# Raw weights asked for five products sooner, and one bank copied out by ScalarE, in the Strassen stage of a hybrid encoder block

## The chip, the cores and the metric

The kernel runs on one core of one Trainium2 chip. The metric is the device time of one execution in microseconds. The core has TensorE (PE, matmuls), VectorE (DVE), ScalarE (ACT), GpSimd (POOL) and SyncE (SP, which here issues nearly all DMAs). Each engine works through a queue of its own in order; they meet through semaphores.

## The reference, cut to what matters

The block takes a sequence of 1024 tokens of width 1024, normalises and modulates it to h, projects h with a wide matrix, runs a gated short convolution (branch a) and a bidirectional gated DeltaNet (branch b), and merges both. For this change only the projections for branch a and the last gates matter:

```
proj = h @ w_in[l]
(a_bg, a_cg, a_x, a_z, q, k, v, z_b, a_raw, b_raw, gate_a_raw, gate_b_raw) = jnp.split(proj, ...)
ya = a_cg * dwconv_centred(a_bg * a_x, conv_a_w[l])
ya = ya * jax.nn.silu(a_z)
ya = ya @ w_pa[l]
...
merged = jax.nn.sigmoid(gate_a_raw) * ya + jax.nn.sigmoid(gate_b_raw) * yb
```

## The kernel before, in words

Weights and h are kept as pairs of a high and a low part, so that one product becomes three matmuls (hi·hi, hi·lo, lo·hi). A projection's 1024 columns are eight tiles of 128 columns.

The DeltaNet part comes first. Then, from about 762 us to 1120 us of the span, the *Strassen stage* computes eighteen pairs of column tiles: for j = 0, 2, 4, 6 the pairs bg, ax, cg, az (`a_bg`, `a_x`, `a_cg`, `a_z`), and then the gates gb2 and gb4. Each pair (class `Pair`) is a 2 x 2 block product done with seven products in place of eight (Strassen-Winograd). A product is 12 matmuls of 128x128 by 128x512. The seven are called S2, A11, S1, S3, A12, A22, S4 after their weight operand; A11 to A22 are quarters of the raw weights, S1 to S4 sums of them (VectorE, line 1308). The pair bg0 has the place "first" and another order of products, the pair gb4 the place "last".

For each product there are these steps:
- `load` (line 1317): SyncE asks for the pair's four raw quarters, 256 KB each, into a ring of eight raw buffers, so two pairs' worth.
- `prep`: the sum, if the operand is one, and ScalarE's copy into the high part (line 1324), both five products ahead (`AHEAD = 5`). `prep` calls `load` when a raw quarter is first needed.
- `rest`: VectorE's subtraction into the low part (line 1331), four products ahead.
- `product` (line 1343): the matmuls. S2 and S3 go to a bank of one pool, S1 and S4 to a bank of another; S3 adds into the bank that already holds S2.
- `after`: what leaves the banks. `e1` is ScalarE's copy of A11's bank (line 1349), `u2` is S2's bank plus `e1` (VectorE, line 1351). TensorE may begin S3 only when `u2` has been read from that bank.

`steps` is the list of all products in order; near its end two entries are exchanged, so that gb4's S2 comes one product sooner, ahead of gb2's S4. The order of every engine's instructions in this stage is the order in which this code issues them. The products of branch a are multiplied together by VectorE into a tile `a`, and SyncE stores it to `y_d` (line 1426), one store per column tile, after the last product of az. In the profile a tile's name has no numbers: `u_bg`, `S_gb`, `wr_gb` stand for `u2_bg0`, `S1_gb4`, `wr_gb4..` and their likes; `whS`, `whiS`, `whA`, `whiA` are high parts, `wlS` and so on low parts.

Of the kernel before, what the change touches and what calls it, by code (L numbers as in the profile page):

```python
# [11 lines left out]
ALU = mybir.AluOpType  # L12
# [19 lines left out]
AHEAD = 5  # L32
# [295 lines left out]
def block(ctx: ExitStack, tc: tile.TileContext, x, c, wada, wadag, badaT, nwT, win, wab, cva, cvq,  # L328
# [3 lines left out]
    V, S, G, Q = (Engine(sched, n, e) for n, e in (("dve", nc.vector), ("act", nc.scalar), ("pool", nc.gpsimd),  # L332
                                                   ("dma", nc.sync)))

    def pool(name, bufs, **kw):
        return ctx.enter_context(tc.tile_pool(name=name, bufs=bufs, **kw))
# [4 lines left out]
    pg = pool("pg", 2, space=PSUM)  # L341
# [899 lines left out]
    V, S, G, Q, PE = nc.vector, nc.scalar, nc.gpsimd, nc.sync, nc.tensor  # L1241
# [4 lines left out]
    def wtile(src, name):  # L1246
        hi = wp.tile([P, KT * P], F32R, tag="whi", name=f"wh_{name}")
        lo = wp.tile([P, KT * P], F32R, tag="wlo", name=f"wl_{name}")
        for q in range(2):
            raw = wp.tile([P, 512], F32, tag="wraw", name=f"wr_{name}_{q}")  # L1250
            Q.dma_start(raw, src[:, ch(q, 512)])
            S.activation(hi[:, ch(q, 512)], raw, AF.Copy)  # L1252
            G.tensor_tensor(lo[:, ch(q, 512)], raw, hi[:, ch(q, 512)].bitcast(F32), ALU.subtract)  # L1253
        return hi, lo
# [35 lines left out]
    class Pair:  # L1290
# [62 lines left out]
        def after(self, n, ps):  # L1353
            u = self.u
            if self.place == "last":
                if n in ("S2", "S3"):
                    self.temp({"S2": "u2", "S3": "u3"}[n], ps, None)
                elif n == "A11":
                    self.temp("e1", ps, None)
                    V.tensor_tensor(u["u3"], u["u3"], u["e1"], ALU.add)  # L1360
                    self.consume(1, 1, self.banks[pc], u["u3"])
                    self.consume(1, 0, self.banks[pg], u["e1"])
                    V.tensor_tensor(u["u2"], u["u2"], u["e1"], ALU.add)
                    V.tensor_tensor(u["u2"], self.banks[pc], u["u2"], ALU.add)
                elif n == "A12":
                    self.consume(0, 0, ps, u["e1"])
                elif n == "S4":
                    self.consume(0, 1, ps, u["u2"])
                return
            first = self.place == "first"  # L1370
            if n == "A11":
                self.temp("e1", ps, None)
            if n == ("S2" if first else "A11"):
                self.temp("u2", self.banks[pg], u["e1"])
                if first:
                    V.tensor_tensor(u["u2"], self.banks[po], u["u2"], ALU.add)
            if n == "S3":
                self.temp("u3", ps, u["e1"])
                self.consume(1, 1, self.banks[pc], u["u3"])
            elif n == "A12":  # L1380
                self.consume(0, 0, ps, u["e1"] if first else None)
            elif n == "A22":
                self.consume(1, 0, ps, u["e1"])
            elif n == ("S1" if first else "S4"):
                self.consume(0, 1, ps, u["u2"])
# [45 lines left out]
    def conv3(acc, b, j, i):  # L1431
        x, c = xpads[b][:, 1 + i : 1 + i + T], cva_t[:, j, i : i + 1]
        if i:
            V.scalar_tensor_tensor(acc, x, c, acc, ALU.mult, ALU.add)
        else:
            V.tensor_scalar(acc, x, c, None, ALU.mult)
# [21 lines left out]
    steps = [(p, n) for p in pairs for n in p.order]  # L1458
# [15 lines left out]
        pairs[0].after(n, early[n])  # L1474
    steps[AHEAD - 1][0].prep(steps[AHEAD - 1][1])
    for i, (p, n) in enumerate(steps):
        if i + AHEAD < len(steps):
            q, k = steps[i + AHEAD]
            q.prep(k)
        if i + AHEAD <= len(steps):  # L1480
            q, k = steps[i + AHEAD - 1]
            q.rest(k)
        p.product(n)
        if late:
            conv3(*late.pop(0))
        if i + 4 == len(steps):
            tctx.close()
            yp = ctx.enter_context(tc.tile_pool(name="yp", bufs=1, reuse_waits="tile", side="right"))
            yhi = [yp.tile([P, T], F32R, name=f"yhi{k}") for k in range(KT)]
            ylo = [yp.tile([P, T], F32R, name=f"ylo{k}") for k in range(KT)]  # L1490
            ws = [wtile(win[G_B + j], f"gb{j}") for j in (6, 7)]
            for k in range(KT):
                Q.dma_start(ylo[k].bitcast(F32), y_d[k])
# [187 lines left out]
def build(nc, arrays, dbg=None, **kw):  # L1681
    aps = {n: nc.dram_tensor(f"in_{n}", a.shape, mybir.dt.from_np(a.dtype), kind="ExternalInput").ap()
           for n, a in arrays.items()}
    out = nc.dram_tensor("out_0_dram", (1, 1024, 1024), F32, kind="ExternalOutput").ap()
    with tile.TileContext(nc, **kw) as tc:
        block(tc, *aps.values(), out, **({"dbg": dbg} if dbg else {}))
# [11 lines left out]
```

## Time and profile before

| | us |
|---|---|
| median of 3 runs (lowest, highest) | 1413.46 (1412.38, 1415.14) |
| the profiled execution's own time | 1415.61 |
| its span, first to last instruction | 1413.9 |
| PE busy | 1369.3 |
| DVE busy | 863.0 |
| ACT busy | 613.1 |
| POOL busy | 479.2 |
| mean granted TensorE clock | 0.991 |

Times inside the profile count from the start of the span. A row of a timeline is: start, duration, engine, line, operation, output and inputs, shapes, count, and in brackets the idle time of the engine before it with what ended it. SPq, ACTq, DVEq and PEq are the engines' sequencers, which issue DMAs and wait for semaphores. A row of the waits is: who waited, for whom, total, times, longest.

### The profile page before, as it was taken

How to read it: one execution, taken by the hardware profiler on the slowest of the kernel's cores; microseconds unless marked ns; L12 is line 12 of the kernel's file. 1: busy time of each engine (PE TensorE's matmuls, PEld its weight loads, DVE VectorE, ACT ScalarE, POOL GpSimd, SP SyncE). 2: the span in 40 equal slices, each digit the busy share in tenths (PEclk: the TensorE clock that was granted, in tenths of full speed). 3: DMA queues.
4: the chain of work that ended last, by engine and by line, in shares of the span. 5: the costliest groups of instructions: out<-in, count | busy, mean ns of one | idle time of the engine just before them, and what ended most of it. 6: DMA issues, size and time to landing. Idle time of an engine off the chain costs nothing.

```text
span 1413.9 us, 22356 instructions
## 1 busy us (share of the span) xinstructions
PE 1369.3 (97%) x8498; PEld 1144.7 (81%) x8498; DVE 863.0 (61%) x1479; ACT 613.1 (43%) x1495; POOL 479.2 (34%) x718
## 2 busy tenths in 40 slices
PE   6899999999999999999998999999998999999998
PEld 5678888887888888888887888888886788888886
DVE  6868175667668675857675766767676354432335
ACT  5447575564647475655534232322323331222211
POOL 2004837574747565665510000000000122455301
PEclk9999999999999999999999999999999999999999
DMA  9315341515042332314223102030301477664502
GB/s 356 97 53 161 112 92 67 150 38 143 31 99 82 83 98 71 109 46 98 54 105 120 59 38 97 16 123 26 120 30 60 172 282 246 217 205 158 178 15 104
DMA packets 124300, 155.96 MB, mean 110 GB/s; under 512 B 74657, under 2 KB 75041, under 8 KB 124194
## 3 DMA queue, kind: packets, MB, share of 16 engines
q1 hardware_dynamic: 123762, 153.24, 33.7%
q8 instruction: 66, 1.08, 0.3%
q10 hardware_dynamic: 432, 1.31, 0.2%
q14 instruction: 40, 0.33, 0.1%
HBM read 125.02 MB, written 29.50 MB: 109 GB/s over the span
## 4 chain that ended last, share of the span: by engine, by line
PE 91%; DVE 4%; DMA 1%; ACT 1%; issue 1%; SPq 0%; POOL 0%; POOLq 0%; DVEq 0%; ACTq 0%
PE pp_ga L214 6%; PE pp_z L214 6%; PE cb L214 6%; PE pp_q L214 5%; PE pp_v L214 5%; PE pp_k L214 5%; PE ps_ax_S L1343 4%; PE ps_cg_S L1343 4%; PE o L214 4%; PE ps_bg_S L1343 4%; PE ps_az_S L1343 4%; PE pp_pb L1261 2%; PE pp_pb L1263 2%; PE pp_pa L1263 2%; PE pp_pa L1262 2%; PE pp_pa L1261 2%
## 5 line engine op out<-in xcount | busy, mean ns | idle before, releaser
L1253 POOL TENSOR_TENSOR wl_gb<-wr_gb,wh_gb 128x512 fp32r<-128x512 f32 x4 | 5.1, 1296 | 360.1 <-ACT wh_gb L1252 360.1
L322 POOL TENSOR_TENSOR E<-E,et 128x30 f32<-128x30 f32 (+7 forms) x240 | 117.0, 488 | 16.8
L322 POOL TENSOR_TENSOR et<-E 128x30 f32<-128x30 f32 (+7 forms) x240 | 112.8, 470 | 29.3 <-DMA E<-s 12.7
L322 DVE SCALAR_TENSOR_TENSOR S<-S,exps,cb 128x128 f32<-128x128 f32 x96 | 29.6, 343 | 59.4 <-PE cb L214 58.8
L322 ACT ACTIVATE vw<-cb,cols 128x128 f32<-128x128 f32 x112 | 36.2, 364 | 68.2 <-PE cb L214 67.9
L214 PE MATMUL pp_z<-hhi,wh_z 128*128 128x512 f32 x128 | 52.8, 412 | 0.0
L214 PE MATMUL pp_z<-hhi,wl_z 128*128 128x512 f32 x128 | 52.7, 412 | 0.0
L214 PE MATMUL pp_z<-hlo,wh_z 128*128 128x512 f32 x128 | 52.7, 412 | 0.0
L214 PE MATMUL pp_ga<-hhi,wh_ga 128*128 128x512 f32 x128 | 51.6, 403 | 0.0
L214 PE MATMUL pp_ga<-hhi,wl_ga 128*128 128x512 f32 x128 | 51.6, 403 | 0.0
L214 PE MATMUL pp_ga<-hlo,wh_ga 128*128 128x512 f32 x128 | 51.5, 402 | 0.0
L1261 PE MATMUL pp_pb<-bhi,wh_pb 128*128 128x512 f32 x128 | 50.4, 394 | 0.0
L322 DVE SCALAR_TENSOR_TENSOR r<-cb,negeg,vp 128x128 f32<-128x128 f32 x112 | 34.5, 345 | 25.8 <-PE cb L214 25.3
L1263 PE MATMUL pp_pb<-bhi,wl_pb 128*128 128x512 f32 x128 | 50.2, 392 | 0.0
L1261 PE MATMUL pp_pa<-yhi,wh_pa 128*128 128x512 f32 x128 | 49.8, 389 | 0.0
L1263 PE MATMUL pp_pa<-yhi,wl_pa 128*128 128x512 f32 x128 | 49.8, 389 | 0.0
L1262 PE MATMUL pp_pa<-ylo,wh_pa 128*128 128x512 f32 x128 | 49.8, 389 | 0.0
L1262 PE MATMUL pp_pb<-blo,wh_pb 128*128 128x512 f32 x128 | 49.7, 388 | 0.0
L322 ACT ACT_TABLE_LOAD x38 | 48.8, 1283 | 1.5 <-PEq L1693 0.8
L322 DVE SCALAR_TENSOR_TENSOR vT<-xpad,cvq_t,vT 128x1024 f32<-128x1024 f32 x32 | 48.9, 1528 | 0.3
L1253 POOL TENSOR_TENSOR wl_pa<-wr_pa,wh_pa 128x512 fp32r<-128x512 f32 x16 | 26.1, 1647 | 67.1 <-ACT wh_pa L1252 59.8
L214 PE MATMUL pp_q<-hhi,wl_q 128*128 128x512 f32 x112 | 44.8, 400 | 3.3 <-issue 3.3
(885 smaller groups left out, 4383.7 us busy)
## 6 DMA issues: line engine op xcount, KB each, us to landing
wada<-in_wada SPq DMA_DIRECT2D x16, 512.0 KB, 8.5
D<-gr_d SPq DMA_DIRECT2D x16, 512.0 KB, 6.8
wr_bg<-in_win SPq DMA_DIRECT2D x18, 256.0 KB, 2.8
xt<-in_x SPq DMA_DIRECT2D x8, 512.0 KB, 8.9
wr_k<-in_win SPq DMA_DIRECT2D x16, 256.0 KB, 2.7
wr_q<-in_win SPq DMA_DIRECT2D x16, 256.0 KB, 2.6
wr_v<-in_win SPq DMA_DIRECT2D x16, 256.0 KB, 3.0
wr_ga<-in_win SPq DMA_DIRECT2D x16, 256.0 KB, 2.7
```

The source lines that it names most:

```text
L214: getattr(self.pe, what)(out, *ins, **kw)
L322: self._sched.record(self._name, lambda: real(*args, **kw), outs, ins, cost, extra, table, op == "memset", port)
L1253: G.tensor_tensor(lo[:, ch(q, 512)], raw, hi[:, ch(q, 512)].bitcast(F32), ALU.subtract)
L1261: PE.matmul(ps, wh, mhi[k][:, sl], start=i == 0, stop=False)
L1262: PE.matmul(ps, wh, mlo[k][:, sl], start=False, stop=False)
L1263: PE.matmul(ps, wl, mhi[k][:, sl], start=False, stop=i == KT - 1)
L1343: PE.matmul(ps, w, r, start=first and m == i == 0, stop=m == 3 and i == 2, skip_group_check=True)
```

## The change

Two edits. The loop over the products now calls `load` for the pair whose product comes ten products later, where `prep` called it five products ahead. And for the pair bg0, `u2` is made in three steps instead of two: ScalarE copies S2's bank, VectorE adds `e1` to the copy, and then S1's bank as before.

```
@@ class Pair, after()
             if n == ("S2" if first else "A11"):
-                self.temp("u2", self.banks[pg], u["e1"])
+                self.temp("u2", self.banks[pg], None if first else u["e1"])
                 if first:
+                    V.tensor_tensor(u["u2"], u["u2"], u["e1"], ALU.add)
                     V.tensor_tensor(u["u2"], self.banks[po], u["u2"], ALU.add)
...
@@ the loop over the products
     for i, (p, n) in enumerate(steps):
+        if i + AHEAD + 5 < len(steps) and not steps[i + AHEAD + 5][0].raw:
+            steps[i + AHEAD + 5][0].load()
         if i + AHEAD < len(steps):
             q, k = steps[i + AHEAD]
             q.prep(k)
```

SyncE's queue differs in four places, once for each j: the loads of the pair after next now stand ahead of the two stores of `y_d`. The last of the four, SyncE before (the `wr_gb` at the head are the last of gb2, those behind the stores are gb4's; `a` are the two tiles of branch a for j = 6):

```order
L1317 DMA wr_gb_10344<-in_win 128x512
L1317 DMA wr_gb_10346<-in_win 128x512
L1426 DMA y_d<-a_10136 128x1024
L1426 DMA y_d<-a_10157 128x1024
L1317 DMA wr_gb_10471<-in_win 128x512
L1317 DMA wr_gb_10473<-in_win 128x512
L1317 DMA wr_gb_10475<-in_win 128x512
L1317 DMA wr_gb_10477<-in_win 128x512
```

SyncE now, at the same place:

```order
L1317 DMA wr_gb_10255<-in_win 128x512
L1317 DMA wr_gb_10257<-in_win 128x512
L1317 DMA wr_gb_10370<-in_win 128x512
L1317 DMA wr_gb_10372<-in_win 128x512
L1317 DMA wr_gb_10374<-in_win 128x512
L1317 DMA wr_gb_10376<-in_win 128x512
L1427 DMA y_d<-a_10145 128x1024
L1427 DMA y_d<-a_10166 128x1024
```

The four loads of gb4 moved ahead of the two stores; for j = 0, 2, 4 it is the four loads of the next ax pair. The order of VectorE, ScalarE and GpSimd is otherwise the same as before, and so is TensorE's.

ScalarE around the first pair, before (`whS_ax` and `whiA_ax` are high parts of ax0's weights, `e_bg` is `e1` of bg0):

```order
L1349 ACTIVATE e_bg_8174<-ps_first_A_8043 128x512
L1324 ACTIVATE whS_ax_8189<-S_ax_8187 128x512
L1324 ACTIVATE whiA_ax_8206<-wr_ax_8181 128x512
L1324 ACTIVATE whiA_ax_8206<-S_ax_8185 128x512
L1324 ACTIVATE whiS_ax_8243<-S_ax_8241 128x512
```

ScalarE now:

```order
L1349 ACTIVATE e_bg_8174<-ps_first_A_8043 128x512
L1324 ACTIVATE whS_ax_8189<-S_ax_8187 128x512
L1324 ACTIVATE whiA_ax_8206<-wr_ax_8181 128x512
L1349 ACTIVATE u_bg_8222<-ps_bg_S_8209 128x512
L1324 ACTIVATE whiA_ax_8206<-S_ax_8185 128x512
L1324 ACTIVATE whiS_ax_8252<-S_ax_8250 128x512
```

The copy `u_bg` came in, between the first and the second `whiA_ax`. VectorE's queue keeps its length there; its first `u_bg` reads the copy and no longer the bank.

More of the change, by code (lines that the diff above doesn't have):

```diff
@@ L1373, in after @@
             if n == ("S2" if first else "A11"):
-                self.temp("u2", self.banks[pg], u["e1"])
+                self.temp("u2", self.banks[pg], None if first else u["e1"])
                 if first:
+                    V.tensor_tensor(u["u2"], u["u2"], u["e1"], ALU.add)
                     V.tensor_tensor(u["u2"], self.banks[po], u["u2"], ALU.add)
@@ L1476, in block @@
     for i, (p, n) in enumerate(steps):
+        if i + AHEAD + 5 < len(steps) and not steps[i + AHEAD + 5][0].raw:
+            steps[i + AHEAD + 5][0].load()
         if i + AHEAD < len(steps):
```

## The prediction

> **What bounds the kernel now.** I read the page first, then the waits of TensorE alone, then the windows around its waits, then the chain of waits and the timelines inside two of them.
>
> From the page, the engines' busy shares and the chain that ended last:
>
> ```profile
> PE 1369.3 (97%) x8498; PEld 1144.7 (81%) x8498; DVE 863.0 (61%) x1479; ACT 613.1 (43%) x1495; POOL 479.2 (34%) x718
> PE 91%; DVE 4%; DMA 1%; ACT 1%; issue 1%; SPq 0%; POOL 0%; POOLq 0%; DVEq 0%; ACTq 0%
> ```
>
> TensorE is the bound. An edit off its path is worth nothing; an edit is worth the TensorE waits that it shortens, plus what the lowered clock costs after them. In the waits of TensorE (total, times, longest), the three inside the Strassen stage are:
>
> ```profile
> PE ps_gb_S L1343 <- DVE u_gb L1351: 5.0, 1, 5.0
> PE ps_bg_S L1343 <- DVE u_bg L1351: 3.7, 1, 3.7
> PE ps_gb_S L1343 <- ACT u_gb L1349: 1.4, 1, 1.4
> ```
>
> The windows table gives, for each stretch, its length and TensorE's busy time; the granted clock stands ahead of the DMA share:
>
> ```profile
> 774.13:779.38 5.25, 5.25 (x12) 4.09 (x13) 2.97 (x5) 0.00 (x0) 0.00 (x0) 0.50 0.28 101
> ...
> 840.00:880.00 40.00, 40.00 (x174) 32.48 (x174) 27.34 (x42) 11.53 (x21) 0.00 (x0) 1.00 0.33 119
> ...
> 1086.37:1091.00 4.63, 4.63 (x12) 3.70 (x13) 2.35 (x4) 2.54 (x3) 0.00 (x0) 0.58 0.02 5
> ```
>
> From 800 to 1080 TensorE is full in every such stretch (one is shown): no load or store there can gain anything. After each of the two long waits the next product (12 matmuls) runs at a clock of 0.50 or 0.58. An undisturbed product takes 2.76, as the last row of the next fence says, so the low clock costs 5.25 - 2.76 = 2.49 us after the first wait and 4.63 - 2.76 = 1.87 after the second.
>
> **The late stall, and the loads.** The chain of waits around the 5.0 us (start, duration, piece):
>
> ```profile
> 1076.80 0.70 DVE a L1424
> ...
> 1077.52 0.33 SPq L1426
> ...
> 1077.90 0.42 SPq L1317
> ...
> 1078.42 0.73 SPq L1317
> ...
> 1079.24 3.98 DMA wr_gb<-in_win
> ...
> 1091.17 2.76 PE ps_gb_A L1343 x12
> ```
>
> The raw weights of gb4 are asked for only at 1077.90, because in SyncE's queue they stand behind the stores of `y_d`, and the second store waits for VectorE's last product into `a`, which ends at 1077.50. The order listing moves exactly these four loads ahead of the two stores. What else holds them? Their raw buffers are those of az6 (eight buffers, four per pair). The timelines of SyncE and VectorE say when those are free:
>
> ```profile
> 1056.95 0.69 DVE L1331 TENSOR_TENSOR wloA_az<-wr_az,whiA_az 128x512 fp32r<-128x512 f32 x1 [1.35 <-ACT whiA_az L1324]
> ...
> 1074.20 3.65 SPq L1426 DMA_DIRECT2D y_d<-a  x2
> ...
> 1077.90 2.22 SPq L1317 DMA_DIRECT2D wr_gb<-in_win  x4
> ...
> DMA to landing us min/median/max: 2.5/3.0/4.0
> ```
>
> The last reader of az6's raw weights ends at 1057.64. So the four loads go out by about 1059 (0.33 to 0.73 for an issue), land by 1063 with the 4.0 of the slowest `wr_gb`, and are wanted by VectorE at 1078. That is 15 us of cover; if it were gone the loads would cost what they cost now. The stores are ready only at 1074.20 and 1077.50, long after the loads left the queue, so being moved behind them costs the stores nothing; the same move for the other three pairs changes DMA times where TensorE is full. I cost all of these at zero.
>
> What is late next? VectorE's and ScalarE's queues in order, and TensorE on both sides of the wait:
>
> ```profile
> 1060.46 0.68 DVE L1308 TENSOR_TENSOR S_gb<-wr_gb,wr_gb 128x512 f32<-128x512 f32 x1
> 1061.18 0.69 DVE L1308 TENSOR_TENSOR S_gb<-S_gb,wr_gb 128x512 f32<-128x512 f32 x1
> ...
> 1077.41 0.68 DVE L1331 TENSOR_TENSOR wloA_gb<-wr_gb,whiA_gb 128x512 fp32r<-128x512 f32 x1
> 1082.28 0.69 DVE L1308 TENSOR_TENSOR S_gb<-wr_gb,wr_gb 128x512 f32<-128x512 f32 x1 [4.18 <-DMA wr_gb<-in_win]
> 1083.67 0.69 DVE L1308 TENSOR_TENSOR S_gb<-S_gb,wr_gb 128x512 f32<-128x512 f32 x1 [0.69 <-DMA wr_gb<-in_win]
> ...
> 1084.47 0.63 ACT L1324 ACTIVATE whiS_gb<-S_gb 128x512 fp32r<-128x512 f32 x1 [7.91 <-DVE S_gb L1308]
> 1085.01 0.58 ACT L1349 ACTIVATE e_gb<-ps_gb_A 128x512 f32<-128x512 f32 x1
> ...
> 1085.62 0.69 DVE L1351 TENSOR_TENSOR u_gb<-ps_gb_S,e_gb 128x512 f32<-128x512 f32 x1 [0.66 <-ACT e_gb L1349]
> ...
> 1080.95 0.40 PE L1343 MATMUL ps_gb_S<-sums,wlS_gb 128*128 128x512 f32 x1
> 1086.37 1.22 PE L1343 MATMUL ps_gb_S<-sums_D,whS_gb 128*128 128x512 f32 x2 [5.02 <-DVE u_gb L1351]
> ```
>
> TensorE's S3 of gb2 adds into the bank that `u_gb` reads, so it must wait for `u_gb`; `u_gb` needs ScalarE's copy `e_gb`; that stands behind `whiS_gb`, which needs the second `S_gb`. Without the DMA wait: the first `S_gb` starts one spacing after 1077.41 (0.61, as from 1076.80 to 1077.41), at 1078.02; the second 0.72 later (as 1060.46 to 1061.18), at 1078.74, ending 1079.43; `whiS_gb` 0.11 after that (as 1084.36 to 1084.47), at 1079.54; `e_gb` 0.54 later at 1080.08, ending 1080.66; `u_gb` at 1080.69, ending 1081.38; TensorE 0.06 later (as 1086.31 to 1086.37), at **1081.44**. By its own rate TensorE would be free at 1080.95 + 0.23 = 1081.18. So a wait of 0.26 us stays, and the start moves by 1086.37 - 1081.44 = **4.93 us**. With the wait that short the clock should hold: the wait of 1.41 us before 1103.56 lowers nothing (fence below). That returns the **1.87 us**. Does the faster product make something new late? The next `u_gb` had waited 2.49 us for that product's end:
>
> ```profile
> 1091.20 0.69 DVE L1351 TENSOR_TENSOR u_gb<-ps_gb_S,e_gb 128x512 f32<-128x512 f32 x1 [2.49 <-PE ps_gb_S L1343]
> ...
> 1103.56:1108.00 4.44, 4.44 (x19) 3.61 (x20) 1.39 (x2) 2.11 (x4) 0.00 (x0) 1.00 0.29 118
> ```
>
> Of these 2.49, 1.87 are used up and 0.62 stay. Sum of this place: 6.80 us.
>
> **The first stall, and the copy.** The timeline there, with one piece of the chain and one later ScalarE copy for comparison:
>
> ```profile
> 769.25 0.58 ACT L1349 ACTIVATE e_bg<-ps_first_A 128x512 f32<-128x512 f32 x1
> ...
> 772.03 0.63 ACT L1324 ACTIVATE whS_ax<-S_ax 128x512 fp32r<-128x512 f32 x1 [2.20 <-DVE S_ax L1308]
> ...
> 773.08 0.61 ACT L1324 ACTIVATE whiA_ax<-S_ax 128x512 fp32r<-128x512 f32 x1
> 773.30 0.68 DVE L1351 TENSOR_TENSOR u_bg<-ps_bg_S,e_bg 128x512 f32<-128x512 f32 x1
> 774.01 0.69 DVE L1376 TENSOR_TENSOR u_bg<-ps_bg_S,u_bg 128x512 f32<-128x512 f32 x1
> ...
> 774.13 1.19 PE L1343 MATMUL ps_bg_S<-sums_D,whS_bg 128*128 128x512 f32 x2 [3.68 <-DVE u_bg L1351]
> ...
> 779.62 0.69 DVE L1351 TENSOR_TENSOR u_bg<-ps_bg_S,e_bg 128x512 f32<-128x512 f32 x1 [2.52 <-PE ps_bg_S L1343]
> ...
> 785.18 2.76 PE ps_ax_A L1343 x12
> ...
> 1102.91 0.60 ACT L1349 ACTIVATE u_gb<-ps_gb_S 128x512 f32<-128x512 f32 x1 [4.33 <-DVE gb L1446]
> ```
>
> The added ScalarE copy takes the slot at 773.08 and, at the 0.58 of the nearest row of its kind (`e_bg`, also bank to SBUF), ends at 773.66; with 0.05 to TensorE (the copy that ends at 1103.51 lets TensorE start at 1103.56) it starts at 773.71 in place of 774.13: 0.42 us earlier. The copy is no earlier because it stands in ScalarE's queue behind `whS_ax`, which waits for `S_ax`, and the first `whiA_ax`. VectorE's adds now wait for the copy: they start 0.4 later and push `wloA_ax`, `xpad`, `S_ax` by as much, into the 2.52 us of idle before 779.62; `whiA_ax` is pushed by 0.6 and its product begins at 785.18. Both cost nothing under that cover; without it, 0.4 to 0.6 each. The idle time of TensorE becomes 3.26 us. In this execution the low clock ended at 779.38. If that end is set by time, 0.42 us more at half speed is worth **0.21 us**; if no clock is lost at all, 0.42 + 2.49 = 2.91; if the copy were as slow as the add, 0. I take 0.21, the value nearest to the row of before, and keep 0 and 2.91 for the range.
>
> Here the Trainium skill has a rule, "TensorE: Matmul & The Clock Gate", section "What's actually happening": the clock goes to half after at least one idle window of about 3.4 us, and the window runs freely. By it a wait of 3.26 could no longer cool the array, and the sum would be 2.7 us larger. The trace agrees that 3.68 cools and 1.41 does not; no row lies between.
>
> **The sum.** 4.93 + 1.87 + 0.21 = 7.01 us. The profiled execution took 1415.61 us (span 1413.9 and 1.7 around it), 2.15 above the median 1413.46 of the runs and a little above their highest, 1415.14; in its own frame the sum gives 1408.6. Stated against the median, 1413.46 - 7.01 = **1406.4**. Behind 1120 TensorE is full again, as in this row of the windows table, and I found no wait there that is set by a clock time of another engine, so I pass the gain through whole:
>
> ```profile
> 1160.00:1200.00 40.00, 40.00 (x178) 33.14 (x177) 20.41 (x19) 7.02 (x10) 12.74 (x8) 1.00 0.71 240
> ```
>
> **The rivals.**
> - *The clock holds at the first stall too.* For it: the idle time falls to 3.26. Against it: half a clock's worth was lost at 3.68, hardly longer. 1413.46 - 6.80 - 2.91 = 1403.75. Chance 0.20. The skill's idle window would make it so.
> - *The late stall shrinks, but u_gb is late for another reason.* Two engines hand over four times in 4.03 us, with no slack; one handover or add that runs 1.2 us late leaves 1.4 us of wait, which the clock survives: 1407.6. [...] Chance 0.14.
> - *The loads do not come sooner.* If a raw buffer were held until 1077, SyncE would ask when it does now; only the copy would be left: 1413.2. Against it: the row at 1056.95. Chance 0.04.
> - *Slower: the loads stand in front of the stores and wait there.* If az6's raw buffers came free at X, behind 1077.90, all that hangs on the loads moves by X - 1077.90, and the stores, now behind them, too; from X = 1080.8 it costs more than 2.8 us, and at X = 1085 the time is 1413.46 + 7.1 = 1420.6. Chance 0.03.
>
> **How the numbers follow.** The forecast itself has 0.59, with its own range from 1404.8 to 1408.4 (the three runs of before spread over 2.8 us). A measurement of this kernel can tell 0.2%, 2.8 us, from no change: below 1410.6 is faster. That takes in the forecast, the clock rival and most of the third: 0.90. Same: 0.07. Slower: 0.03. The 8-in-10 range reaches from just under the clock rival, 1403.2, to the late-u_gb case with some clock lost, 1409.4.
>
> **What would show it.** In the profile after: the four `wr_gb` loads issued before 1062 and the two `y_d` stores still at about 1074 and 1077; no DMA wait ahead of `S_gb`; TensorE's wait for `u_gb` near 0.1 on the waits view and a granted clock of 1.00 in the product behind it; the wait at 774 about 3.3 and named for ScalarE; the 1.4 unchanged. A wait of over 1 us at 1081, or a load still behind a buffer, would prove the sum wrong; a full clock behind the first wait would put it 2.7 us too high.

## The result and the profile after

| | before | after |
|---|---|---|
| median (lowest to highest), us | 1413.39 (1411.97 to 1415.14) | 1405.37 (1403.98 to 1409.65) |
| executions | 6 | 6 |
| the profiled execution's own time, us | 1415.61 | 1405.5 |
| its span, us | 1413.9 | 1403.8 |
| mean granted TensorE clock | 0.991 | 0.994 |

The ratio of after to before is 0.9945, with a 95% interval from 0.9929 to 0.996: faster by 8.0 us, where the interval stands for 5.7 to 10.0. The forecast was 1406.4, with a range from 1403.2 to 1409.4. One execution of the kernel with VectorE reordered (see the table of experiments) took 1743.7 us at a granted clock of 0.734; the cause is not known, and it is left out of that kernel's median and ratio. The page of after, busy shares and the chain that ended last:

```profile
PE 1366.0 (97%) x8498; PEld 1142.7 (81%) x8498; DVE 860.7 (61%) x1479; ACT 613.9 (44%) x1496; POOL 480.1 (34%) x718
PE 92%; DVE 4%; DMA 1%; ACT 1%; issue 1%; SPq 0%; POOL 0%; POOLq 0%; ACTq 0%; DVEq 0%
```

TensorE is still the bound. Its waits inside the Strassen stage (who, for whom, total, times, longest), after:

```profile
PE ps_bg_S L1343 <- ACT u_bg L1349: 3.3, 1, 3.3
...
PE ps_gb_S L1343 <- ACT u_gb L1349: 1.4, 1, 1.4
...
PE ps_gb_S L1343 <- DVE u_gb L1351: 0.4, 1, 0.4
```

The 5.0 has become 0.4, the 3.7 has become 3.3 and is named for ScalarE, and the 1.4 stands. SyncE's timeline of after at the place where the loads stood behind the stores:

```profile
1026.39 27.85 SPq L1317 DMA_DIRECT2D wr_gb<-in_win  x8
1070.46 3.65 SPq L1427 DMA_DIRECT2D y_d<-a  x2
```

All eight loads of gb2 and gb4 are out by 1026.39 + 27.85 = 1054.24, 16 us ahead of the stores. VectorE, ScalarE and TensorE of after around the late stall:

```profile
1074.99 0.69 DVE L1308 TENSOR_TENSOR S_gb<-S_gb,wr_gb 128x512 f32<-128x512 f32 x1
...
1076.09 0.63 ACT L1324 ACTIVATE whiS_gb<-S_gb 128x512 fp32r<-128x512 f32 x1 [3.27 <-DVE S_gb L1308]
1076.63 0.58 ACT L1349 ACTIVATE e_gb<-ps_gb_A 128x512 f32<-128x512 f32 x1
...
1077.24 0.69 DVE L1351 TENSOR_TENSOR u_gb<-ps_gb_S,e_gb 128x512 f32<-128x512 f32 x1 [0.96 <-ACT e_gb L1349]
...
1077.20 0.40 PE L1343 MATMUL ps_gb_S<-sums,wlS_gb 128*128 128x512 f32 x1
1077.99 0.73 PE L1343 MATMUL ps_gb_S<-sums_D,whS_gb 128*128 128x512 f32 x2 [0.40 <-DVE u_gb L1351]
```

No row waits for a DMA any more. And the windows of after, one for the product behind each of the two stalls (length, TensorE's busy time and count, then the other engines, the granted clock, DMA share, GB/s):

```profile
771.50:775.91 4.41, 4.41 (x12) 3.52 (x13) 3.77 (x6) 0.47 (x1) 0.00 (x0) 0.62 0.04 6
...
1077.99:1080.88 2.89, 2.89 (x12) 2.36 (x13) 2.35 (x4) 1.64 (x3) 0.00 (x0) 1.00 0.03 6
```

The late product runs at the full clock, 2.89 us; the one behind the first stall still at 0.62, 4.41 us.

**A measure that leaves the front out.** The two spans differ by 10.1 us, more than the medians do. What stands ahead of the stage takes a different time in each execution; TensorE's first matmul of bg0 in this stage, before and then after:

```profile
761.96 0.47 PE L1343 MATMUL ps_bg_S<-hhi,wh_S 128*128 128x512 f32 x1 [0.86 <-DVE sz L322]
```

```profile
759.75 0.47 PE L1343 MATMUL ps_bg_S<-hhi,wh_S 128*128 128x512 f32 x1 [0.85 <-DVE sz L322]
```

From here to the end of the span it is 1413.9 - 761.96 = 651.94 us before and 1403.8 - 759.75 = 644.05 after. I call this the *tail*. A second profiled execution of the changed kernel gave 644.01, so the tail repeats far better than the total, and it is given for each kernel below, from one profiled execution each. The gain of 7.89 us in the tail lies here:

| place | before, us | after, us | gain |
|---|---|---|---|
| first stall, start of S1's last matmul to start of S3 | 4.07 | 3.65 | 0.42 |
| bg0's S3, low clock | 5.25 | 4.41 | 0.84 |
| from there to the late stall | 301.57 | 301.29 | 0.28 |
| late stall, start to start | 5.42 | 0.79 | 4.63 |
| gb2's S3 | 4.63 | 2.89 | 1.74 |

Behind gb2's S3 the rest of the span is 322.90 us before and 322.92 after, so the gain passes through whole. That isn't so in every kernel below: it is 323.49 with the loads alone and 323.25 with the copy one place ahead, because TensorE's product into `pp_pa` near 1137 comes late there (with the loads alone its row names VectorE's `ylo`). Such a loss is in the tail, too.

### The profile page after: what moved, and what is told of

The parts are those of the page before. It is cut to its first block, busy times and chain, and to the rows that moved or that the text cites. A ratio compares the mean times of both kernels' runs of the same rounds, so it can differ in the third digit from the quotient of the medians.

```text
span 1403.8 us, 22367 instructions
## 1 busy us (share of the span) xinstructions
PE 1366.0 (97%) x8498; PEld 1142.7 (81%) x8498; DVE 860.7 (61%) x1479; ACT 613.9 (44%) x1496; POOL 480.1 (34%) x718
## 4 chain that ended last, share of the span: by engine, by line
PE 92%; DVE 4%; DMA 1%; ACT 1%; issue 1%; SPq 0%; POOL 0%; POOLq 0%; ACTq 0%; DVEq 0%
PE pp_ga L214 6%; PE pp_z L214 6%; PE cb L214 6%; PE pp_q L214 5%; PE pp_v L214 5%; PE pp_k L214 5%; PE ps_ax_S L1343 4%; PE ps_cg_S L1343 4%; PE o L214 4%; PE ps_az_S L1343 4%; PE ps_bg_S L1343 3%; PE pp_pb L1261 2%; PE pp_pb L1263 2%; PE pp_pa L1261 2%; PE pp_pa L1262 2%; PE pp_pa L1263 2%
## 5 line engine op out<-in xcount | busy, mean ns | idle before, releaser
L322 POOL TENSOR_TENSOR et<-E 128x30 f32<-128x30 f32 (+7 forms) x240 | 109.9, 458 | 29.0 <-DMA E<-s 12.4
```

Of the source, the lines that this page charges most:

```text
L322: self._sched.record(self._name, lambda: real(*args, **kw), outs, ins, cost, extra, table, op == "memset", port)
```

## The experiments

Medians are of the executions on the same chip as the kernel before; the ratio is to before, with its 95% interval. "bg0's S3" is the length of the product behind the first stall, "late" is the idle time ahead of gb2's S3 that the timeline names.

| kernel | median, us | ratio [interval] | tail, us | bg0's S3, us | late, us |
|---|---|---|---|---|---|
| before (first profile) | 1413.39 | | 651.94 | 5.25 | 5.02 |
| after | 1405.37 | 0.9945 [0.9929, 0.996] | 644.05 | 4.41 | 0.40 |
| copy only | 1411.96 | 0.9997 [0.9986, 1.0007] | 650.31 | 4.44 | 4.59 |
| loads only | 1405.96 | 0.9943 [0.993, 0.9956] | 644.76 | 4.41 | none named |
| loads two products sooner | 1406.0 | 0.9947 [0.9933, 0.996] | 645.12 | 2.90 | 2.06 |
| loads three products sooner | 1405.34 | 0.9947 [0.9932, 0.9962] | 644.01 | 4.45 | 0.38 |
| copy, stores on GpSimd's queue | 1404.2 | 0.9939 [0.9926, 0.9953] | 644.19 | 4.44 | 0.37 |
| copy one place ahead | 1405.15 | 0.9943 [0.993, 0.9955] | 642.04 | 2.90 | none named |
| copy ahead of whS_ax | 1401.29 | 0.9917 [0.9902, 0.9932] | 640.85 | 2.90 | none named |
| two buffers for u2 | 1401.88 | 0.9928 [0.9913, 0.9943] | 642.41 | 4.40 | 0.37 |
| after, again | 1405.93 | 0.9947 [0.9932, 0.9963] | 644.01 | 4.43 | 0.38 |
| early copy and two buffers | 1399.24 | 0.9906 [0.9888, 0.9925] | 639.10 | 2.91 | none named |
| the same, VectorE reordered | 1399.88 | 0.99 [0.9882, 0.9919] | 637.67 | 2.91 | none named |
| after, one ScalarE copy twice | 1407.35 (one execution) | | 644.00 | 4.45 | 0.36 |

**Each edit alone.** First the loads, with the copy left out:

```
 after(): self.temp("u2", self.banks[pg], u["e1"])        # as before
 loop:    the two lines with AHEAD + 5 stay
```

> The first edit alone: raw weights asked for ten products ahead, u2 of the first pair made by VectorE from the bank as before. My sum: the late wait of TensorE falls from 5.0 us to 0.4 as in the changed kernel and the product behind it runs at full clock, so 6.4 to 6.8 us faster than before (about 1406.8). The wait at 774 stays 3.7 us, ended by VectorE's u_bg, with some 5 us of low clock behind it. Rival (the copy brings a large share): only 4 us or less faster than before.

And the copy, with the two lines of the loop left out:

> The second edit alone: loads asked for as before. My sum: TensorE waits 3.3 us instead of 3.7 at the first stall, 0.2 to 1.3 us faster than before according to where the low clock ends (1412 to 1413.2, not to be told from before); the late wait stays 5.0 us and ends on VectorE's u_gb behind the DMA of wr_gb. Rival (the clock holds because the wait is shorter): 2.9 us faster, with a granted clock of 1.00 in the product behind the wait.

The loads alone bring 0.9943, which the medians do not tell from both edits; in the tail they bring 651.94 - 644.76 = 7.18 of the 7.89. The copy alone cannot be told from no change by its median. The copy's kernel still has the late stall, and SyncE's timeline and TensorE's row say why (SyncE first):

```profile
1069.86 3.65 SPq L1427 DMA_DIRECT2D y_d<-a  x2
1073.56 2.23 SPq L1317 DMA_DIRECT2D wr_gb<-in_win  x4
```

```profile
1081.58 1.16 PE L1343 MATMUL ps_gb_S<-sums_D,whS_gb 128*128 128x512 f32 x2 [4.59 <-DVE u_gb L1351]
```

The loads stand behind the second store, as before the change. In the kernel with the loads alone the same place reads (two rows of TensorE's timeline):

```profile
1077.91 0.40 PE L1343 MATMUL ps_gb_S<-sums,wlS_gb 128*128 128x512 f32 x1
1078.40 0.73 PE L1343 MATMUL ps_gb_S<-sums_D,whS_gb 128*128 128x512 f32 x2
```

**Is it the distance or the place in the queue?** The loads asked for two and three products sooner, in place of five:

```
-        if i + AHEAD + 5 < len(steps) and not steps[i + AHEAD + 5][0].raw:
-            steps[i + AHEAD + 5][0].load()
+        if i + AHEAD + 2 < len(steps) and not steps[i + AHEAD + 2][0].raw:     # or + 3
+            steps[i + AHEAD + 2][0].load()
```

> As the changed kernel, but the raw weights are asked for seven products ahead instead of ten. In SyncE's queue the four loads of gb4 then stand between the two stores of y_d, behind the first, which is ready 3.3 us before the second. If the place in the queue decides: the loads go out about 3.3 us sooner than before, TensorE's late wait falls from 5.0 to about 1.7 us, too short to lower the clock, and the kernel is about 1.3 us slower than the changed one (1406.7). If the number of products ahead decides, as the words of the change say: two of five steps, so about 40 per cent of the gain, some 3 us faster than before (1410.5).

> As the changed kernel, but asked for eight products ahead. The loads of gb4 stand ahead of both stores, as in the changed kernel (those of the three ax pairs between the stores). If the place in the queue decides: the same time as the changed kernel (1405.4, within its spread), late wait 0.4 us. If the number of products ahead decides: 60 per cent of the gain, 1408.6.

With two, the loads fall between the two stores. SyncE's and TensorE's timelines of that kernel:

```profile
1069.59 0.33 SPq L1427 DMA_DIRECT2D y_d<-a  x1
1069.98 2.26 SPq L1317 DMA_DIRECT2D wr_gb<-in_win  x4
1072.91 0.33 SPq L1427 DMA_DIRECT2D y_d<-a  x1
```

```profile
1078.80 0.73 PE L1343 MATMUL ps_gb_S<-sums_D,whS_gb 128*128 128x512 f32 x2 [2.06 <-DVE u_gb L1351]
```

So two fifths of the late stall are there, 2.06 us where 1.7 was expected, as if one of the two stores held the loads. (The tail of this kernel, 645.12, is flattered: its product behind the first stall ran in 2.90 us and not in some 4.4, behind an idle time no shorter.) With three they pass both stores and the wait is 0.38, as with five. The times agree: if the distance decided, they would be 1410.5 and 1408.6, and the upper ends of the intervals (0.996 and 0.9962 of 1413.15, before's median beside these runs) are 1407.5 and 1407.8. To take the stores away altogether, the next kernel has the copy but not the early loads, and issues the stores from GpSimd:

```
-                Q.dma_start(y_d[j0 + b], a)
+                G.dma_start(y_d[j0 + b], a)
...
-        if i + AHEAD + 5 < len(steps) and not steps[i + AHEAD + 5][0].raw:
-            steps[i + AHEAD + 5][0].load()
```

> The copy by ScalarE as in the change, the raw weights asked for where they were asked before it (no early loads), and the eight stores of y_d issued on GpSimd's queue, so that on SyncE's queue nothing stands between the raw loads of the Strassen stage and these stores any more. Theory of the queue (the transfers were late because they stood behind two stores that wait for gb's A22 and S2 results in SyncE's in-order queue): the wr_gb loads leave as soon as their buffers are free, at the latest near 1061 us, the wait of 4.6 us at gb's S3 falls under 0.8 us, and the time is 1405 to 1407, the same as the change's 1405.4. Rival (it is the distance of five products that brings the gain): no change from the kernel with the copy alone, 1411 to 1413. Third: GpSimd waits at the stores and delivers its own work later; then a new wait of some us stands at another product and the time is above 1408.

SyncE's timeline of this kernel, then GpSimd's, then TensorE's row:

```profile
1024.67 27.85 SPq L1317 DMA_DIRECT2D wr_gb<-in_win  x8
1086.24 0.33 SPq L1452 DMA_DIRECT2D sgb_d<-gb  x1
```

```profile
1069.00 0.53 POOL L1427 DMA_DIRECT2D y_d<-a  x1 [73.55 <-DVE a L1425]
1072.44 0.54 POOL L1427 DMA_DIRECT2D y_d<-a  x1 [2.91 <-DVE a L1425]
```

```profile
1076.24 0.73 PE L1343 MATMUL ps_gb_S<-sums_D,whS_gb 128*128 128x512 f32 x2 [0.37 <-DVE u_gb L1351]
```

The loads go out as they do with the change, without being asked for any sooner in the program, and tail (644.19) and late wait (0.37) are those of the change. GpSimd stood idle for 73.55 us ahead of its store, until VectorE's `a` was there (it is `a` that the stores wait for, not gb's products, as the expectation says), and among TensorE's waits no new one appears. The distance of five products is not what brings the gain; that the loads no longer stand behind two waiting stores is.

**The first stall.** The copy put one place ahead on ScalarE, in front of the first `whiA_ax`:

```
 after(), bg0's S2:  self.temp("u2", self.banks[pg], None)
+                    q, k = steps[1 + AHEAD]
+                    q.prep(k)
 loop:
-        if i + AHEAD < len(steps):
+        if i != 1 and i + AHEAD < len(steps):
```

> The change, with the copy of S2's bank moved one place ahead on ScalarE, in front of the first whiA_ax (0.61 us). The idle of TensorE ahead of bg's S3 goes from 3.27 us to 2.6 to 2.8. Theory A (the low clock of the product behind it depends on the length of the idle, and 2.7 us is short of what brings it): the 12 matmuls take 2.9 us in place of 4.4, and the time falls by 0.6 + 1.5 = 2.1 to about 1403.3. Theory B (any idle over some 2 us can bring it): they take 4.4 again and the time falls by 0.6 at most, 1404.8. The late wait stays at 0.1 to 0.5 us in both.

TensorE's timeline and the window of the product behind it:

```profile
772.29 0.73 PE L1343 MATMUL ps_bg_S<-sums_D,whS_bg 128*128 128x512 f32 x2 [2.74 <-ACT u_bg L1349]
```

```profile
772.29:775.19 2.90, 2.90 (x12) 2.37 (x13) 2.80 (x6) 0.99 (x2) 0.00 (x0) 1.00 0.01 3
```

The idle time fell by 0.53, the clock held, and the tail fell by 2.0, as theory A has it (2.1); the stall and the product behind it account for 0.52 + 1.51. This is one profiled execution. The medians (1405.15 and 1405.37) do not show these 2 us: the executions of one kernel spread over 3 to 6 us. Then the copy put further ahead, directly behind `e_bg`, with `whS_ax` and `wlS_ax` behind it:

```
 after(), bg0's S2:  self.temp("u2", self.banks[pg], None)
+                    q, k = steps[AHEAD - 1]
+                    q.prep(k)
+                    q.rest(k)
+                    q, k = steps[1 + AHEAD]
+                    q.prep(k)
 ahead of the loop:
-    steps[AHEAD - 1][0].prep(steps[AHEAD - 1][1])
+    steps[AHEAD - 1][0].operand(steps[AHEAD - 1][1])
```

> The change, with the copy of S2's bank put in front of whS_ax and wlS_ax on ScalarE and VectorE, directly behind the copy e_bg. The copy then needs only S2's last matmul and the start of ScalarE, so the idle of 3.27 us ahead of bg's S3 falls to 0.1 to 0.9 us and the product runs in 2.9 us in place of 4.4. If nothing else is late: 2.4 to 3.2 + 1.5 = 3.9 to 4.7 us, time 1400.7 to 1401.5. Rival: what was moved behind the copy is needed by ax's S2 three products on; then a wait of 0.5 to 1.5 us stands there and the time is 1401.5 to 1403. Rival two: the idle is bounded by VectorE's addition for the bank and not by the copy, time unchanged at 1405.4.

TensorE's timeline: S1's last matmul, S3's first, and the first of bg0's A22 (ax0's S2 runs between S3 and A22, since `steps` has a second exchange, near its start):

```profile
763.85 0.39 PE L1343 MATMUL ps_bg_S<-sums,wl_S 128*128 128x512 f32 x1
764.15 0.73 PE L1343 MATMUL ps_bg_S<-sums_D,whS_bg 128*128 128x512 f32 x2
...
771.62 0.73 PE L1343 MATMUL ps_bg_S<-sums_N,wh_S 128*128 128x512 f32 x2 [1.61 <-DVE u_bg L1351]
```

The first stall is gone (0.30 from start to start, in place of 3.65), the product takes 2.90, and a new wait of 1.61 us stands ahead of A22. The tail fell by 3.20, less than the 3.9 to 4.7 expected. The rival had a wait of 0.5 to 1.5 at ax0's S2; it came at another product and for another reason. VectorE's rows in this kernel: the sum `u_bg` from S3's bank (line 1351) stands behind `S_ax` and `wloA_ax`, though S3 ended near 767.

```profile
769.68 0.68 DVE L1308 TENSOR_TENSOR S_ax<-wr_ax,wr_ax 128x512 f32<-128x512 f32 x1
770.28 0.69 DVE L1331 TENSOR_TENSOR wloA_ax<-S_ax,whiA_ax 128x512 fp32r<-128x512 f32 x1
770.88 0.69 DVE L1351 TENSOR_TENSOR u_bg<-ps_bg_S,e_bg 128x512 f32<-128x512 f32 x1
```

**The wait of 1.4.** The tile `u2` has one buffer; with two:

```
-            t = self.u[k] = btile(k, f"{k}_{self.name}", 1)
+            t = self.u[k] = btile(k, f"{k}_{self.name}", 2 if k == "u2" else 1)
```

> The change with two buffers in place of one for the tile that holds the copy of S2. In the trace of the changed kernel a wait of 1.41 us ahead of gb's S3's second group ends with ScalarE's copy u_gb, which had to wait for the buffer of bg. With a second buffer the copy can start as soon as S2's bank is full. Theory (the buffer is the bound): that wait goes, and the time falls by up to 1.4 us, to about 1404.0. Rival (ScalarE is busy or the bank is late then): the wait stays within 0.3 us of 1.4, time 1405.4.

ScalarE's copy in after, and then with two buffers:

```profile
1092.80 0.60 ACT L1349 ACTIVATE u_gb<-ps_gb_S 128x512 f32<-128x512 f32 x1 [4.34 <-DVE gb L1447]
```

```profile
1087.87 0.60 ACT L1349 ACTIVATE u_gb<-ps_gb_S 128x512 f32<-128x512 f32 x1 [0.84 <-PE ps_gb_S L1343]
```

In after the copy for gb4 waits until VectorE's `gb` has read the u2 of gb2 from the only buffer (the expectation says bg; it is the pair before). With two it waits for TensorE alone, the wait of 1.4 is gone, and the tail falls by 1.64. The median fell by 3.5, but the intervals of the two kernels overlap; the tail gives the size, since the totals spread too far for it.

**Together.** The changed kernel again, beside the two versions that put these together:

> The changed kernel unaltered, to have its time beside the two versions below on the same chip, and a second profiled execution of it. By the first: 1404 to 1407. At the first stall the first profile had an idle of 3.27 us and a product of 4.4 us behind it; if the loss of clock at such an idle varies between executions, this product may also come out at 2.9 us, with the same idle.

> The change, with the early copy (S2's bank copied by ScalarE directly behind e_bg, ahead of whS_ax) and two buffers for u2. If the two act at separate places, as the traces say, their gains add: the early copy took 3.0 us off the stretch from bg0's S1 to ax0's A11, the second buffer took 1.6 us off gb4's place. Expected 1405.4 - 4.6 = 1400.8; by the medians of the two runs (4.1 and 3.5 under the change) 1397.8. Rival (they share one limit): 1401.3, as the early copy alone. The wait of 1.6 us ahead of bg0's A22, ended by VectorE's u_bg, should be there again.

> As the one before, and on VectorE bg0's u3 (the sum read from S3's bank, u_bg, for which bg0's A22 waits) is put ahead of S_ax and of both wloA_ax, which nobody needs for another 3 us. Theory (VectorE's order made the wait of 1.6 us ahead of A22): that wait goes to under 0.2 us and nothing else moves, 1.6 us less than the one before, 1396.2 to 1399.2. Rival (wloA_ax and S_ax are then late for ax0's A11 and S1): a wait of 0.5 to 1.5 us moves there, and the gain over the one before is under 1 us.

In the last one the loop lets bg0's S1 and S3 go out ahead of the preparations that stood in front of them:

```
+        if i in (2, 3):
+            p.product(n)
+        if i == 3:
+            q, k = steps[i + AHEAD - 2]
+            q.rest(k)
...
-        if i and i + AHEAD <= len(steps):
+        if i not in (0, 2) and i + AHEAD <= len(steps):
...
-        p.product(n)
+        if i not in (2, 3):
+            p.product(n)
```

Early copy and second buffer add: 644.05 - 639.10 = 4.95 us of tail, against 3.20 and 1.64 singly. The wait of 1.61 ahead of A22 is there again:

```profile
PE ps_bg_S L1343 <- DVE u_bg L1351: 1.6, 1, 1.6
```

With VectorE reordered no wait for `u_bg` is left among TensorE's waits, and the tail is 1.43 us shorter still, near the 1.6 expected: A22 starts at 776.40, still 0.16 later than TensorE's own spacing would have it. VectorE's row in that kernel, S3's `u_bg` now ahead of `wloA_ax` and `S_ax`:

```profile
775.67 0.68 DVE L1351 TENSOR_TENSOR u_bg<-ps_bg_S,e_bg 128x512 f32<-128x512 f32 x1
...
776.99 0.68 DVE L1331 TENSOR_TENSOR wloA_ax<-wr_ax,whiA_ax 128x512 fp32r<-128x512 f32 x1
```

The medians, 1399.24 and 1399.88, do not separate these two. Both have their intervals wholly under that of the change.

**One ScalarE copy twice.** This was aimed at the 0.3 us by which the late handover was longer than forecast:

```
         q.prep(k)
+            if i == 40:
+                hi, _, t = q.ops[k]
+                S.activation(hi, t, AF.Copy)
```

> The changed kernel with one ScalarE copy of branch a's middle pairs done twice (40 products into the stage, where ScalarE waits for work). It is to tell where the 0.3 us come from by which whiS_gb starts later behind S_gb than predicted (0.41 in place of 0.11), and with it TensorE at the late stall. Theory (it hangs on where the instruction stands in ScalarE's program): the handover changes to 0.1, and the wait at the late stall falls from 0.4 to 0.1. Rival (it is something else that goes with the copy's place): it stays at 0.4.

The rival holds: `whiS_gb` starts at 1077.95, 0.39 behind the end of `S_gb` (1076.87 + 0.69).

## Why the prediction was right, point by point

- *The loads and the stores.* Right for gb4, in each part. The loads go out when az6's raw buffers are free: the forecast's 1057.64 for the last reader, moved by the 3.75 us that after is ahead at that place (1080.95 to 1077.20), gives 1053.9; in after that reader (VectorE's `wloA_az`) ends at 1053.19 + 0.69 = 1053.88, and the last issue of SyncE's row ended at 1054.24. The stores were not delayed: they start at 1070.46, 3.74 ahead of before.
- *The other three pairs.* The forecast costed their earlier loads at zero, since TensorE looked full from 800 to 1080. One of them was worth a little. In before, VectorE waits 1.66 and 1.02 us for the DMAs of `wr_ax` near 927, `u_bg` of j = 4 ends only at 930.91 + 0.69 = 931.60, and TensorE's A22 of that pair starts at 931.65, 0.13 later than its spacing, and takes 2.91 in place of after's 2.80: 0.24 in all. The kernel with the copy alone has the same place as a named wait of 0.25 for `u_bg`. In after VectorE waits for no DMA there, and `u_bg` is done 1.88 us ahead of A22.
- *The rest of the late wait.* The forecast had 1081.44 - 1080.95 = 0.49 us from the last matmul's start to S3's start; after has 0.79. The term that was mis-sized is the handover from `S_gb` to `whiS_gb`: 0.11 in the forecast, 1076.09 - (1074.99 + 0.69) = 0.41 in after. With the loads alone the two rows above give 1078.40 - 1077.91 = 0.49, the forecast to the hundredth, with a handover of 0.12. The handover is 0.39 to 0.41 in all six profiled executions with the copy in the change's place and no store ahead of the loads, and 0.11 to 0.12 in all five with early loads in which the copy is absent or stands further ahead on ScalarE. What links a copy at 770 with a handover at 1076 stays open; adding a ScalarE instruction in between did not move it.
- *The clock at the late stall.* 1.87 forecast, 1.74 measured. The clock is back at 1.00; the product takes 2.89, not the 2.76 that the chain gave for a later product.
- *The copy.* TensorE's idle time became 3.27, forecast 3.26, and ends with ScalarE's `u_bg` as forecast. The gain at the stall is 0.42. The forecast put the copy at 0.21 with the clock's share, and the profile shows 0.42 + 0.84 = 1.26 at this place. But the 0.84 is not the copy's: with the loads alone the idle time is 3.69 as before, and the product still takes 4.41. It was before's profiled execution that lost more clock than any other here (5.25). So the copy is worth 0.42 there, of which the longer handover that goes with it takes 0.30 back at the late stall, and its own effect is far under what the medians can tell, as the ratio 0.9997 of the copy alone says.
- *The sum.* Late place 4.63 + 1.74 = 6.37 against 6.80; first place 0.42 against 0.21; 6.8 against 7.0. The 0.21 came from halving the 0.42, as if the low clock ended at a fixed time; but the product takes 4.41 both with the copy and with the loads alone, so the low clock moved along with TensorE's start, and the whole 0.42 counts. That the sum comes so near is partly luck: the late place was 0.43 too high, the first stall 0.21 and the other pairs 0.24 too low. The remaining 0.84 of the tail is the large loss of clock in before's profile. Of the 0.28 between the stalls, 0.24 is the place of j = 4 above (the stretch is 301.29 with the loads alone and with both edits, and 301.71 with the copy alone); the rest is within what the end of the low clock explains, since in before the product behind bg0's S3 (779.38 to 782.29) still has a clock of 0.96 and takes 2.91, and in after 1.00 and 2.80.
- *The rivals.* That the loads would not come sooner, or would hold back the stores, is refuted by SyncE's rows. That `u_gb` is late for another reason came true on a small scale, 0.3 in place of 1.2 us. The clock rival did not come true in after; it did in the kernel with the loads two products sooner, where bg0's S3 took 2.90 behind the same idle time, so at this length the clock can go either way. The upper end of the range counts some clock as lost behind a longer late wait; no run shows from which length on: it held behind 2.06 us there and was lost behind 4.59 with the copy alone.

## What to carry to other kernels

On an in-order DMA queue, look at what stands in front of a load and what that waits for: a store that waits for the last result of a stage holds back every load behind it, and moving either one, by three products or to another queue, was worth nearly the whole gain here. When such a stall goes, the waits it hid become the next ones; copying a bank out sooner, a second buffer and another order on VectorE took a further 6.4 us off the tail. And judge an edit of 1 to 3 us by the stretch behind the last thing that varies (here 644.00 to 644.05 in two profiles of the changed kernel and in those of two kernels that do the same work in the same places), since totals that spread over 3 to 6 us don't show it; look behind the stretch as well, where 0.3 to 0.6 us can be lost again.

## What the runs showed of the hardware

- *The clock behind an idle time just over 3 us.* Idle times of 3.26 to 3.31 us ahead of bg0's S3 lowered the clock in seven profiled executions (the product took 4.40 to 4.45 us) and did not in one, with 3.31, where it took 2.90; 3.68 and 3.69 lowered it in both of theirs. The windows of the one:

```profile
771.34:774.24 2.90, 2.90 (x12) 2.36 (x13) 2.80 (x5) 0.47 (x1) 0.00 (x0) 1.00 0.01 3
```

 Idle times of 2.74 and 2.06 us (one profiled execution each) and of 1.6 us (two) did not lower it. The Trainium skill, "TensorE: Matmul & The Clock Gate", section "What's actually happening", has the clock fall after at least one idle window of about 3.4 us, of a window that runs freely. By the idle times that the profile shows the trace disagrees: seven of eight fell at less than that. Measured from S1's last matmul plus one spacing of 0.23 to S3's start (767.85 + 0.23 to 771.50 in after) the gap is 3.42 us, right at the window's length; but a window that runs freely would seldom lie wholly inside such a gap, and most fell.
- *How long the low clock lasts.* In after the first 3.49 us of the product have a granted clock of 0.52 and what follows has 1.00:

```profile
771.50:774.99 3.49, 3.49 (x8) 2.77 (x9) 3.39 (x6) 0.47 (x1) 0.00 (x0) 0.52 0.01 2
774.99:778.71 3.72, 3.72 (x17) 3.01 (x16) 1.76 (x3) 0.00 (x0) 0.00 (x0) 1.00 0.41 141
```

 A loss costs 4.41 - 2.90 = 1.5 us, and in before's profile 5.25 - 2.90 = 2.35. So 0.5 us off an idle time that is near this border brought 2.0 us in the tail in the one execution that was profiled (the copy one place ahead).
